# Strassen-type weight sums for the second FFN, made in HBM by accumulating transfers of GpSimd's queue

## The chip, the cores and the metric

The kernel runs on one core of one Trainium2 chip. The metric is the device time of one execution in microseconds (us); several runs are given by their median. TensorE multiplies a stationary operand of 128 x 128 with a moving operand of up to 512 columns into a bank of PSUM. VectorE (DVE), ScalarE (ACT) and GpSimd (POOL) work on tiles of 128 partitions. Transfers are issued by the queues of SyncE (SP), ScalarE and GpSimd and carried out by sixteen DMA engines. Each engine takes its instructions in the order in which the built program has them.

## The reference

Two layers over 256 tokens of width 2048 in float32. Layer 0 mixes tokens by latent attention, layer 1 by dilated attention; each is followed by an FFN whose up projection has 2 x 5632 columns and a causal convolution of width 3.

```python
def conv_ffn(h, w_up, conv_w, conv_b, w_down):
    u = h @ w_up
    up = jnp.pad(u, ((0, 0), (CONV_WIDTH - 1, 0), (0, 0)))
    c = conv_b + up[:, 0:S] * conv_w[0]
    for j in range(1, CONV_WIDTH):
        c = c + up[:, j:j + S] * conv_w[j]
    gate, val = c[..., :FFN_HIDDEN], c[..., FFN_HIDDEN:]
    return (jax.nn.silu(gate) * val) @ w_down

for i in range(DEPTH):
    x = x + (mla_mixer if i % 2 == 0 else dilated_mixer)(rms_norm(x, attn_norm[i]), ...)
    x = x + conv_ffn(rms_norm(x, ffn_norm[i]), ffn_w_up[i], ...)
return rms_norm(x, final_norm)
```

## The kernel before, in words

Activations are kept transposed: 16 chunks `xt[k]` of 128 features by 256 tokens. Every float32 operand is split into a high and a low part (`wh`, `wl` for weights, `xs` for activations), and a product is the sum of three: high by high, low by high, high by low.

A **unit** is one block of 128 output features. `load` brings 1 MB of weights on SP's queue into one of three buffers `w`, ScalarE makes `wh` and VectorE `wl` (tiles of 1024 columns, five buffers each), and `proj` runs 16 matmuls of 512 columns (`wh` by high and low of `xs`) and 16 of 256 (`wl` by the high part). `unit` evacuates the bank of the unit before and takes one entry of `steps`, a list of other work laid between units.

The norm's factor is applied after the product: `rstd_x` sums squares with TensorE, and GpSimd takes the power to -1/2 (`rcol`). `spread` then has TensorE make a table over all partitions from it. In `ffn` the steps `col` and `wide` do so beside the first units; `keep` multiplies by that table, writes the result into one of four padded tiles `upad`, which GpSimd clears at their first two columns, and calls `conv`. In the first mixer, GpSimd also adds the squares of x (`acc`) and takes the powers for the two latent norms (`s`).

The FFN has 44 feature blocks `fb`, each with a gate and a value unit (`up`). Their outputs stay in SBUF for a segment (`SEGS`) of 10 to 12 blocks, then `down` runs 16 units, one for each output chunk, over that segment.

A **four** is a group of four consecutive blocks that is not computed directly. `seven` treats tokens (two halves), input features (two halves) and gate or value as a 2 x 2 x 2 block product and does it with seven products in place of eight, after Winograd's form. The roles are turned: 128 tokens are stationary, and 512 columns of weights move. A product has 8 x 3 matmuls. The stationary sums (`forms`, from `make_forms`) are made once; the weight sums `t13` and `t24` are made on VectorE. Six products advance together, one slice of the input features at a time (`first`, `second`), between the units of a `down`; the seventh (`third`), the sums of the outputs and the transposes back (`turn`) follow as steps of the next units. There are three fours (`SEVEN`, at 12, 23 and 34) in each of the two FFNs.

The built order is not the order of the text: a scheduler places each instruction on its engine by its dependences and by its own estimate of times, within the buffers that are free.

## Time and profile before

| | us |
|---|---|
| three runs | 2674.88, 2675.78, 2676.62 |
| median | 2675.78 |
| profiled execution, first to last instruction (span) | 2673.9 |
| first mixer, up to GpSimd's power for the first FFN's norm | 272 |
| first FFN | 722 |
| second mixer (dilated attention and its output projection) | 951 |
| second FFN | 719 |

Only the span is known of the profiled execution; it lies 1.9 us below the runs' median. The stages are cut at GpSimd's powers, of which there is one for each norm. In the profile, a row of an engine names its line, its operation and its tiles as output<-inputs.

### The profile page before, as it was taken

To read this page: it belongs to the slowest core of one execution; us is meant where nothing else is said; L and a number is where in the kernel's file an instruction comes from. 1 tells how busy PE (TensorE), PEld (TensorE's weight loads), DVE (VectorE), ACT (ScalarE), POOL (GpSimd) and SP (SyncE) were. 2 spreads that over 40 slices of the span, in tenths; PEclk is the share of its full clock that TensorE was granted. 3 is DMA by queue.
4 is the path that set the end of the run, shared out by engine and by line. 5 is a ranking of instruction groups with operands and counts; after the bars stand their busy time and mean duration, and the time that the engine had idled before them with its cause. 6 is when DMAs were issued, how large, how long until landed. Compare 5 with 4: busy or idle time off the path is not lost.

```text
span 2673.9 us, 40017 instructions
## 1 busy us (share of the span) xinstructions
PE 2657.8 (99%) x15167; PEld 2338.4 (87%) x15167; DVE 2105.5 (79%) x3630; ACT 1639.7 (61%) x2624; POOL 24.7 (1%) x39
## 2 busy tenths in 40 slices
PE   9999999999999999999999999999999999999998
PEld 7998888888888888898888888888888888888887
DVE  7987888898898876676577667667688889889885
ACT  6775666676666764444454444445666667666665
POOL 2000000000000000000000000000000000000000
PEclk9999999999999999999999999999999999999999
DMA  6335555656566565544544544544555575755744
GB/s 246 138 133 203 189 182 193 239 179 224 197 202 227 182 206 198 179 171 170 191 170 164 197 161 174 188 174 160 189 189 175 191 249 171 223 205 189 237 169 147
DMA packets 153553, 506.19 MB, mean 189 GB/s; under 512 B 11024, under 2 KB 86160, under 8 KB 118928
## 3 DMA queue, kind: packets, MB, share of 16 engines
q1 hardware_dynamic: 153072, 503.46, 54.9%
q8 instruction: 119, 1.95, 0.3%
q14 instruction: 74, 0.61, 0.1%
q10 hardware_dynamic: 288, 0.18, 0.0%
HBM read 501.50 MB, written 2.10 MB: 188 GB/s over the span
## 4 chain that ended last, share of the span: by engine, by line
PE 95%; DMA 1%; DVE 1%; issue 0%; ACT 0%; SPq 0%; DVEq 0%; ACTq 0%
PE pp L137 70%; PE pp L165 3%; PE pp L167 3%; PE pp L166 3%; PE ps L855 1%; PE ps L853 1%; PE ps L854 1%; DMA w<-in_wup 1%; PE pp L104 1%; PE pp L106 1%; PE pp L105 1%; PE pp L853 1%; PE pp L854 1%; PE pp L855 1%; PE po L781 1%; PE ps L744 1%
## 5 line engine op out<-in xcount | busy, mean ns | idle before, releaser
L92 DVE TENSOR_TENSOR wl<-w,wh 128x1024 fp32r<-128x1024 f32 (+3 forms) x802 | 881.9, 1110 | 371.0 <-ACT wh L91 228.1
L91 ACT ACTIVATE wh<-w 128x1024 fp32r<-128x1024 f32 (+3 forms) x802 | 770.9, 966 | 370.8 <-PE pp L137 220.7
L137 PE MATMUL pp<-xs,wh 128*128 128x512 f32 x3648 | 855.5, 390 | 0.0
L137 PEld LDWEIGHTS pp<-xs,wh 128*128 128x128 f32 x3648 | 677.1, 188 | 135.8 <-DVE xs L266 0.2
L137 PE MATMUL pp<-xs,wl 128*128 128x256 f32 x3648 | 465.3, 284 | 0.0
L137 PEld LDWEIGHTS pp<-xs,wl 128*128 128x128 f32 x3648 | 455.7, 191 | 9.3
L137 PE MATMUL pp<-a,wh 128*128 128x512 f32 x1920 | 459.7, 390 | 0.0
L137 PEld LDWEIGHTS pp<-a,wh 128*128 128x128 f32 x1920 | 357.7, 188 | 72.6
L137 PEld LDWEIGHTS pp<-a,wl 128*128 128x128 f32 x1920 | 248.1, 191 | 10.2
L137 PE MATMUL pp<-a,wl 128*128 128x256 f32 x1920 | 252.8, 283 | 0.0
L155 DVE TENSOR_TENSOR wl<-w,wh 128x1024 fp32r<-128x1024 f32 x96 | 116.2, 1218 | 62.3 <-ACT wh L154 50.3
L154 ACT ACTIVATE wh<-w 128x1024 fp32r<-128x1024 f32 x96 | 101.6, 1059 | 96.5 <-PE pp L166 50.0
L213 ACT ACTIVATE lo<-pp 128x256 f32<-128x256 f32 x225 | 85.7, 381 | 119.5 <-PE pp L137 119.4
L165 PE MATMUL pp<-wh,xs 128*128 128x512 f32 x384 | 150.0, 391 | 0.0
L167 PE MATMUL pp<-wl,xs 128*128 128x512 f32 x384 | 149.5, 389 | 0.0
L166 PE MATMUL pp<-wh,xs 128*128 128x512 f32 x384 | 149.4, 389 | 0.0
L962 DVE SCALAR_TENSOR_TENSOR cv<-upad,convs,cv 128x256 f32<-128x256 f32 x256 | 121.1, 481 | 18.3 <-ACT cv L958 15.9
L958 ACT ACTIVATE cv<-upad,convs 128x256 f32<-128x256 f32 x128 | 76.4, 598 | 72.7 <-DVE upad L972 71.0
L215 DVE TENSOR_TENSOR sum<-pp,lo 128x256 f32<-128x256 f32 x225 | 94.1, 418 | 0.2
L120 ACT ACTIVATE pp<-x 128x512 f32<-128x512 f32 x144 | 85.1, 591 | 13.6 <-DVE sum L215 6.8
L880 ACT ACTIVATE wh<-w 128x1024 fp32r<-128x1024 f32 x48 | 51.0, 1062 | 60.0 <-PE pp L137 43.0
L167 PEld LDWEIGHTS pp<-wl,xs 128*128 128x128 f32 x384 | 72.1, 188 | 15.0
(299 smaller groups left out, 3154.7 us busy)
## 6 DMA issues: line engine op xcount, KB each, us to landing
w<-in_wup SPq DMA_DIRECT2D x128, 1024.0 KB, 4.8
w<-in_win SPq DMA_DIRECT2D x96, 1024.0 KB, 4.8
w<-in_wup SPq DMA_DIRECT2D x96, 512.0 KB, 5.1
w<-in_win SPq DMA_DIRECT2D x96, 512.0 KB, 4.1
w<-in_wdn SPq DMA_DIRECT2D x64, 704.0 KB, 4.1
w<-in_wdn SPq DMA_DIRECT2D x32, 768.0 KB, 4.2
w<-in_wdn SPq DMA_DIRECT2D x32, 640.0 KB, 5.3
w<-in_wo SPq DMA_DIRECT2D x16, 1024.0 KB, 4.7
```

The lines of the kernel that those rows point to most:

```text
L91: nc.scalar.activation(h, w[:, c:e], AF.Copy)
L92: nc.vector.tensor_sub(l, w[:, c:e], h.bitcast(F32))
L120: nc.scalar.activation(dst, chunk.unsqueeze(1).to_broadcast([P, 2, 2, P]), AF.Copy, scale=0.5)
L137: nc.tensor.matmul(ps[:, i * T:], w_k, xs[k][:, :(2 - i) * T], start=(k == 0 and i == own), stop=(k == n - 1), skip_group_check=(i != own))
L154: nc.scalar.activation(wh4, src, AF.Copy)
L155: nc.vector.tensor_sub(wl4, src, wh4.bitcast(F32))
L165: nc.tensor.matmul(ps, xh, wh, start=k == 0, stop=False)
L166: nc.tensor.matmul(ps, xl, wh, start=False, stop=False)
L167: nc.tensor.matmul(ps, xh, wl, start=False, stop=k == KC - 1)
L213: nc.scalar.activation(t, ps[:, T:], AF.Copy)
L215: nc.vector.tensor_add(u, ps[:, :T], t)
L962: nc.vector.scalar_tensor_tensor(o, v, convs[:, cw + j:cw + j + 1], o, op0=ALU.mult, op1=ALU.add)
```

## The change

The second layer's FFN gets a function of its own, `ffn_ahead`, with six fours (24 blocks) in place of three. The form of the sums is changed so that the four weight sums are plain additions: with the unit weights w(h, j), where h is gate (0) or value (1) and j the half of the input features, t1 = w(0,0) + w(1,0), t3 = w(1,1) + w(1,0), t2 = w(1,1) + t1, t4 = w(0,1) + t2. Here j halves the 16 chunks as first and last eight, not as even and odd ones. The signs are carried by the stationary forms and the sums of the outputs.

The weight sums are tiles in HBM. `plan_sums` lists, for each four, 16 copies and 16 accumulating transfers (`accum_op=ALU.add`) of 128 x 1024 elements on GpSimd's queue, 192 in all. In the text of `dilated`, two of them are issued with each load of the second mixer, and what is left ahead of its output projection. The products are run one after the other, each in two halves: a half loads 1 MB, either of plain weights or of a ready sum, splits it on ScalarE and VectorE and runs 24 matmuls. `PERIODS` and `steady` lay the halves between the units of three down segments and some direct blocks; the fourth segment follows the last four.

```diff
+FIRST, LAST = 12, 29
+PERIODS = ((0, 11, 12, (16, 17, 18), 19), (11, 18, 23, (27, 28, 29), 30), (18, 29, 34, (38, 39), 40))
...
+        hbm = ctx.enter_context(tc.tile_pool(name="hbm", bufs=1, space=bass.MemoryType.DRAM))
...
+        def plan_sums(layer, fb0):
+            unit_ = lambda f, h, j: wup_d[layer, 2 * (fb0 + f) + h, :, j * WS:(j + 1) * WS]
+            t = {i: hbm.tile([4, P, WS], F32, name=f"t{i}_{layer}_{fb0}") for i in (1, 2, 3, 4)}
+            made[layer, fb0] = t
+            for i, h, j in ((1, 0, 0), (3, 1, 1), (2, 1, 1), (4, 0, 1)):
+                for f in range(4):
+                    sums_ahead.append(lambda i=i, f=f, h=h, j=j: nc.gpsimd.dma_start(t[i][f], unit_(f, h, j)))
+            for i in (1, 3):
+                for f in range(4):
+                    sums_ahead.append(lambda i=i, f=f: nc.gpsimd.dma_start(t[i][f], unit_(f, 1, 0), accum_op=ALU.add))
+            for i, o in ((2, 1), (4, 2)):
+                for f in range(4):
+                    sums_ahead.append(lambda i=i, o=o, f=f: nc.gpsimd.dma_start(t[i][f], t[o][f], accum_op=ALU.add, max_dma_last_dim=WS))
+
+        def some_sums(n):
+            for _ in range(n):
+                if sums_ahead:
+                    sums_ahead.pop(0)()
...
                             w = load(win_d[base + 2 * i + e], D, tok=D)
+                            if j > 0 or g > 0:
+                                some_sums(2)
                             unit(lambda: proj(w, xs, KC), lambda ps, what=what, g=g, e=e: keep_qk((what, g, e), ps))
...
+            some_sums(len(sums_ahead))
             out_proj(dwo_d, os, G_FFN + KC, onto=True)
...
+        def ffn_ahead(layer, goff, ready):
...
+                def product(i, q):
+                    name, what = products[i]
+                    if q == 0:
+                        ps[i] = pss.tile([P, 512], F32, name="ps", tag="ps")
+                    w = wst.tile([P, D], F32, name="w", tag="w")
+                    if isinstance(what, int):
+                        src = t[what][:, :, q * HALF:(q + 1) * HALF]
+                    else:
+                        h, j = what
+                        src = wup_d[layer, 2 * fb0:2 * fb0 + 8].rearrange("(f i) p c -> i f p c", i=2)[h]
+                        src = src[:, :, j * WS + q * HALF:j * WS + (q + 1) * HALF]
+                    nc.sync.dma_start(w.rearrange("p (f c) -> p f c", f=4), src.rearrange("f p c -> p f c"))
+                    w5 = w.rearrange("p (f k c) -> p k f c", f=4, k=4)
+                    for h in range(2):
...
+                        nc.scalar.activation(as4(wh), w5[:, 2 * h:2 * h + 2], AF.Copy)
+                        nc.vector.tensor_sub(as4(wl), w5[:, 2 * h:2 * h + 2], as4(wh).bitcast(F32))
+                        for k in range(2):
...
+                            nc.tensor.matmul(ps[i], xh, bh, start=(kk == 0), stop=False)
+                            nc.tensor.matmul(ps[i], xl, bh, start=False, stop=False)
+                            nc.tensor.matmul(ps[i], xh, bl, start=False, stop=(kk == KC // 2 - 1))
...
+            for fb in range(FIRST):
+                up(fb)
+            for a, b, one, singles, two in PERIODS:
+                am, a_end = seven(one)
+                bm, b_end = seven(two)
+                slots = steady(am, a_end, bm, 2 * len(singles), before)
+                down(a, b)
+                for fb in singles:
+                    up(fb)
+                before = b_end
+            flush()
+            for move in before:
+                move()
+            down(LAST, FB, True)
+            flush()
...
+            for _, _, one, _, two in PERIODS:
+                plan_sums(1, one)
+                plan_sums(1, two)
             dilated()
...
-            ffn(1, G_FFN + KC, final)
+            ffn_ahead(1, G_FFN + KC, final)
```

How the change moves instructions shows on GpSimd first. This is GpSimd's order before, from the last sum of squares of x in the first mixer to the power for the second mixer; the brackets name the semaphores that a row waits for.

```order
L261 TENSOR_TENSOR acc_227<-acc_227,sq_413 128x256 [waits Activation_49]
L309 TENSOR_TENSOR rcol_536<-ms_534,negh_115 128x2 [waits DVE_49]
L321 TENSOR_TENSOR s2_546<-ms_543,negh_115 128x2 [waits DVE_49]
L321 TENSOR_TENSOR s2_759<-ms_756,negh_115 128x2 [waits DVE_49]
L802 MEMSET upad0_3600 128x2 [waits DMAHW6_49,PE_49,Activation_49]
L802 MEMSET upad1_3602 128x2
L802 MEMSET upad2_3604 128x2
L802 MEMSET upad3_3606 128x2
L309 TENSOR_TENSOR rcol_3656<-ms_3654,negh_115 128x2 [waits DVE_49]
L309 TENSOR_TENSOR rcol_11065<-ms_11063,negh_115 128x2 [waits DVE_49]
```

All ten rows are short, and none waits for a transfer of GpSimd's own queue, which has none. Now the same place on GpSimd, at the power for the first mixer's norm; `t1_1_12` is the sum t1 of layer 1's four at block 12, and DMASW0 to DMASW7 are the eight semaphores of GpSimd's transfers.

```order
L206 DMA t1_1_12_11017<-in_wup 128x1024 [waits DMASW1_49]
L285 TENSOR_TENSOR acc_229<-acc_229,sq_415 128x256 [waits Activation_49]
L206 DMA t1_1_12_11017<-in_wup 128x1024 [waits DMASW2_49]
L333 TENSOR_TENSOR rcol_538<-ms_536,negh_117 128x2 [waits DVE_49]
L206 DMA t1_1_12_11017<-in_wup 128x1024 [waits DMASW3_49]
L206 DMA t3_1_12_11019<-in_wup 128x1024 [waits DMASW4_49]
L206 DMA t3_1_12_11019<-in_wup 128x1024 [waits DMASW5_49]
L206 DMA t3_1_12_11019<-in_wup 128x1024 [waits DMASW6_49]
L345 TENSOR_TENSOR s2_548<-ms_545,negh_117 128x2 [waits DVE_49]
L206 DMA t3_1_12_11019<-in_wup 128x1024 [waits DMASW7_49]
L209 DMA t2_1_12_11018<-t1_1_12_11017 512x256 [waits DMASW0_49]
L209 DMA t2_1_12_11018<-t1_1_12_11017 512x256 [waits DMASW1_49]
```

The transfers for the second FFN have moved to the front of the program, between the first mixer's own instructions on GpSimd; four copies stand ahead of the first square, and 19 transfers ahead of this rcol. Further on, GpSimd's order around the power for the first FFN's norm (row 9 of the order before):

```order
L209 DMA t2_1_34_11034<-t1_1_34_11033 512x256 [waits DMASW2_49]
L209 DMA t2_1_34_11034<-t1_1_34_11033 512x256 [waits DMASW3_49]
L209 DMA t4_1_34_11036<-t2_1_34_11034 512x256 [waits DMASW4_49,DMASW0_49]
L209 DMA t4_1_34_11036<-t2_1_34_11034 512x256 [waits DMASW5_49,DMASW1_49]
L209 DMA t4_1_34_11036<-t2_1_34_11034 512x256 [waits DMASW6_49,DMASW2_49]
L209 DMA t4_1_34_11036<-t2_1_34_11034 512x256 [waits DMASW7_49,DMASW3_49]
L203 DMA t1_1_40_11037<-in_wup 128x1024
L333 TENSOR_TENSOR rcol_3658<-ms_3656,negh_117 128x2 [waits DVE_49]
L203 DMA t1_1_40_11037<-in_wup 128x1024 x3
```

Ahead of this power there are now 161 of the 192 transfers: five fours, and the first copy of the sixth. The upad memsets, ahead of it too, stand behind 108 of them. On TensorE, the spread of this power keeps its place at the end of the first FFN's second unit, where it waits for GpSimd.

The other place is TensorE's at the end of the last four. Before, the transposes (outputs `pt` and `po`) stand among direct units (`xs`):

```order
L137 MATMUL pp<-xs_19786,wl 128x256
L137 MATMUL pp<-xs_19795,wl 128x256
L947 MATMUL pt<-cst,t_25705 128x128 [waits DVE_49,PE_49,Activation_49]
L947 MATMUL pt<-cst,t_25705 128x128
L947 MATMUL pt<-cst,t_25704 128x128 x2
L947 MATMUL po<-cst,t_25705 128x128 [waits DVE_49,PE_49,Activation_49]
L947 MATMUL po<-cst,t_25705 128x128
L947 MATMUL po<-cst,t_25704 128x128 x2
L137 MATMUL pp<-xs_19041,wl 128x256
```

Now they follow the last product (`forms`) at once, with only matmuls of the last down segment (`a`) between:

```order
L904 MATMUL ps<-wh,forms_21427 128x512
L905 MATMUL ps<-wl,forms_21427 128x512
L140 MATMUL pp<-a,wh 128x512 [waits Activation_49]
L140 MATMUL pp<-a,wh 128x512 x7
L949 MATMUL pt<-cst,t_25969 128x128 [waits Activation_49]
L949 MATMUL pt<-cst,t_25969 128x128
L949 MATMUL po<-cst,t_25969 128x128 x2
L140 MATMUL pp<-a,wh 128x512 x3
L140 MATMUL pp<-a,wl 128x256 [waits DVE_49]
L140 MATMUL pp<-a,wl 128x256 x7
L140 MATMUL pp<-a,wh 128x512 [waits Activation_49]
```

What moved here is the last four itself: no direct unit stands behind its products any more, and the down segment behind it needs its blocks 40 to 43.

170 lines of the change are left out of this document (added).

## The prediction

> **What bounds the kernel now.** I read the page first, then busy time by stage, then GpSimd's instructions in order of time, and last TensorE's instructions in one stretch of the second layer's FFN.
>
> ```profile
> span 2673.9 us, 40017 instructions
> PE 2657.8 (99%) x15167; PEld 2338.4 (87%) x15167; DVE 2105.5 (79%) x3630; ACT 1639.7 (61%) x2624; POOL 24.7 (1%) x39
> HBM read 501.50 MB, written 2.10 MB: 188 GB/s over the span
> ```
>
> TensorE is at work 99% of the span, so it is the bound, and every wait of TensorE shows in the time one for one. GpSimd has 39 instructions; the kernel writes almost nothing to HBM.
>
> ```profile
> core 0: us, PE busy (x) PEld busy (x) DVE busy (x) ACT busy (x) POOL busy (x), PEclk, DMA share, GB/s
> 0.00:32.00 32.00, 27.34 (x139) 21.17 (x140) 21.29 (x29) 23.12 (x46) 14.34 (x24) 1.00 0.85 305
> ...
> 1945.00:2664.00 719.00, 718.12 (x3994) 627.49 (x3993) 609.10 (x940) 488.85 (x771) 1.77 (x2) 1.00 0.58 195
> ...
> 0.00:64.19 64.19, 58.19 (x324) 48.48 (x325) 50.12 (x88) 45.82 (x84) 17.14 (x26) 1.00 0.68 245
> 64.19:272.03 207.84, 207.54 (x1511) 196.05 (x1510) 170.19 (x453) 138.96 (x340) 1.79 (x6) 1.00 0.45 161
> 0.00:272.03 272.03, 265.73 (x1832) 244.53 (x1833) 220.31 (x540) 184.78 (x424) 18.93 (x32) 1.00 0.51 181
> 272.03:993.99 721.96, 721.96 (x4019) 632.01 (x4018) 622.57 (x963) 496.20 (x780) 1.61 (x1) 1.00 0.60 202
> ```
>
> The last two columns are the busy share of the sixteen DMA engines and what they moved. Up to 272.03 us, which is the whole first mixer, they were busy 0.51 x 272 = 139 us and moved 181 / 0.51 = 355 GB/s while busy (305 / 0.85 = 359 in the fullest stretch). So 133 us of DMA time are free there.
>
> ```profile
> 44.91 0.82 POOL L309 TENSOR_TENSOR rcol<-ms,negh 128x2 f32<-128x2 f32 x1 [11.63 <-DVE ms L307]
> 50.00 0.69 POOL L321 TENSOR_TENSOR s<-ms,negh 128x2 f32<-128x2 f32 x1 [4.27 <-DVE ms L319]
> 64.19 1.59 POOL L321 TENSOR_TENSOR s<-ms,negh 128x2 f32<-128x2 f32 x1 [13.49 <-DVE ms L319]
> 186.78 0.20 POOL L802 MEMSET upad<- 128x2 f32 x4 [120.99 <-ACT a L352]
> 272.03 1.61 POOL L309 TENSOR_TENSOR rcol<-ms,negh 128x2 f32<-128x2 f32 x1 [85.06 <-DVE ms L307]
> ...
> 277.26 0.61 PE L296 MATMUL po<-cst,rcol 128*128 128x128 f32 x4
> ```
>
> These are GpSimd's powers (the norms' reciprocal roots) and, in the last row, TensorE's spread of the one at 272.03, 5.2 us later. All that GpSimd does is short, and TensorE stands behind it within a few us.
>
> **TensorE in the second FFN.** Prices come from starts, since the durations of pipelined matmuls overlap.
>
> ```profile
> 2126.54 0.40 PE L853 MATMUL pp<-wh,forms 128*128 128x512 f32 x1
> ...
> 2127.93 2.43 PE L137 MATMUL pp<-a,wh 128*128 128x512 f32 x10
> 2130.19 1.36 PE L137 MATMUL pp<-a,wl 128*128 128x256 f32 x10
> 2131.38 0.40 PE L853 MATMUL ps<-wh,xs 128*128 128x512 f32 x1
> ...
> 2134.13 2.43 PE L137 MATMUL pp<-a,wh 128*128 128x512 f32 x10
> ...
> L947 PE MATMUL po<-cst,t 128*128 128x128 f32 x24 | 3.6, 273 | 0.0
> L947 PE MATMUL pt<-cst,t 128*128 128x128 f32 x24 | 3.6, 272 | 0.0
> ```
>
> A direct unit is 16 matmuls of 512 columns (2.26 / 10 = 0.226 us each) and 16 of 256 (1.19 / 10 = 0.119): 5.52 us. A matmul of the products takes (2134.13 - 2131.38) / 12 = 0.229 us. Three fours more turn 24 direct units into 504 product matmuls and 48 transposes: -24 x 5.52 = -132.5, +504 x 0.229 = +115.4, +7.2. That is **-10 us**, all on the path, as TensorE is busy 718.12 of 719 us there.
>
> The sums leave VectorE, where they were hidden. A four now takes 28 passes of 1024 columns on each of VectorE and ScalarE; the old products took 44 and 28, four direct blocks 16 and 16.
>
> ```profile
> L882 ACT ACTIVATE wh<-t 128x1024 fp32r<-128x1024 f32 x24 | 25.3, 1054 | 11.0 <-DVE t L881 9.4 <-PE pp L137 1.5
> L895 DVE TENSOR_TENSOR wl<-t,wh 128x1024 fp32r<-128x1024 f32 x24 | 29.3, 1220 | 3.6 <-ACT wh L894 3.6
> ```
>
> VectorE: 6 x 28 - 3 x 44 - 3 x 16 = -12 passes, -15 us, with 110 us to spare in that stage before; ScalarE +36 passes, +38 us, with 230 to spare. Loads of a four stay near 1 MB per 24 product matmuls, 5.5 us, against 1 MB per direct unit of 5.5 us. SP's loads of the sums wait for transfers that landed over 1000 us before. All this I cost at nothing; if the sums were late there, SP and all loads behind it would stand.
>
> One place is new: the last four (blocks 40 to 43) ends straight ahead of the last down segment, where before it ended among direct units. After the last product, VectorE has the sums of the outputs and, for four blocks, the convolutions and splits:
>
> ```profile
> L962 DVE SCALAR_TENSOR_TENSOR cv<-pt,convs,cv 128x254 f32<-128x254 f32 (+1 forms) x24 | 11.4, 477 | 2.0 <-ACT cv L958 2.0
> L967 DVE TENSOR_TENSOR cv<-cv 128x256 f32<-128x256 f32 x44 | 18.5, 420 | 0.6
> L353 DVE TENSOR_TENSOR a<-cv,a 128x256 fp32r<-128x256 f32 x44 | 18.4, 419 | 0.9 <-ACT a L352 0.9
> ```
>
> 4 x (4 x 0.477 + 0.420 + 0.419) = 11 us, against about 6 us of down matmuls that the order puts between the transposes (22 of 512 columns, 11 of 256). Between 0 (more matmuls slip in) and 10 us lost; I take **+5**.
>
> **The sums on GpSimd's queue.** This decides. The code issues them two per load in the second mixer, but they depend on nothing but each other, and in the built order they stand at the front of the program: 160 of the 192 transfers, five fours complete, and one more stand ahead of the first FFN's rcol (272.03 us above). From the ninth on nearly every one waits for an earlier one to land, and GpSimd's queue is in order, so the rcol waits until all but the last five have landed: 80 copies and 76 accumulations of 128 x 1024 x 4 B = 0.524 MB. TensorE's spread waits for the rcol, every later matmul stands behind it, and the loads stop once their buffers are full. On the way the same holds for the squares of the first projection and the powers at 44.91, 50.00 and 64.19 us, but their waits are part of the same lateness: while TensorE stands, the sums go on.
>
> So the rcol comes when the DMA engines have done 139 us of loads and the 156 transfers. The trace has no transfer from HBM to HBM and no accumulation; its nearest rows are loads and stores:
>
> ```profile
> w<-in_wup SPq DMA_DIRECT2D x128, 1024.0 KB, 4.8
> w<-in_wup SPq DMA_DIRECT2D x96, 512.0 KB, 5.1
> out_y<-x SPq DMA_DIRECT2D x7, 256.0 KB, 2.4
> ```
>
> A store has a price like a load's, so three readings bound the sums, all at 355 GB/s. *Each transfer once*: 156 x 0.524 = 81.8 MB, 230 us; the rcol at 139 + 230 = 369, 97 us late. *Each byte read*: an accumulation reads two operands, 80 x 0.524 + 76 x 1.049 = 121.6 MB, 343 us; 210 us late. *Each HBM byte read or written*: 80 x 1.049 + 76 x 1.573 = 203.4 MB, 573 us; 440 us late. The first is too kind, since an accumulation must read what it adds to; between the other two nothing in the trace decides, and I take the middle, **+325 us**.
>
> The Trainium skill, "DMA: Bandwidth & Descriptors", section "Latency and other measured facts", gives 214 GB/s per direction as the full rate of copies between HBM tensors. If an accumulation cost the same, an estimate by that page is 156 x 2.45 = 382 us and the rcol 249 us late; no run here shows such a copy yet.
>
> The other 36 transfers run in the first FFN beside loads that take 0.60 of the DMA time. Hidden as long as the loads, two buffers ahead, still land in time; cost 0 to 20 us, I take **+5**.
>
> The upad memsets at 186.78 us also move behind 108 transfers; their readers need the rcol first, so nothing is added.
>
> Sum: 2673.9 + 325 - 10 + 5 + 5 = 2999 us for the profiled span; the runs' median of 2675.78 lies 2 us above the span: **3000 us**.
>
> **The rivals.** *GpSimd keeps up (faster).* The sums would have to fit into the 133 us that the DMA engines are free before 272 us: 0.85 us for each of 156, or 615 GB/s on top of the loads. Then only -10 + 5 remain: 2671 us. GpSimd's own 1% speaks for it; that the busiest stretch moved 305 GB/s at a share of 0.85 speaks against. It decides at 0.85 us per transfer.
> The same page of the Trainium skill, section "Issuing engines are not separate DMA queues", says that transfers share the sixteen engines whichever engine issued them; by that rule this rival falls. No row shows two busy queues together.
>
> *Cheap sums.* An accumulation costs one pass, 97 us late: 2676 + 97 - 10 = 2763 us. For it: a store as quick as a load. Against: two reads.
>
> *A chain.* Transfers go nearly one at a time, since the last eight of a four wait on the ones just ahead. At the 5.1 us in which 512 KB landed, 156 take 796 us, 524 late: 3200 us. For it: the waits in the order. Against: up to eight may be under way.
>
> **How the numbers follow.** Forecast (late by 210 to 440 us) 0.67, its own range 2885 to 3136; cheap sums 0.13; a chain or worse 0.15; GpSimd keeps up 0.05. The range for 8 in 10 runs from cheap sums to the chain, 2760 to 3200, and leaves out the faster case and half of the chain's. A change under 0.2% (5.4 us) can't be told from none here: the faster rival's 2671 lies at that bound, so 0.03 faster and 0.02 the same; slower 0.95.
>
> **What would show it.** The first FFN's rcol at about 600 us instead of 272; one wait of TensorE of 150 us or more at the spread of rcol, and shorter ones in the first 70 us; DMA busy near 0.9 until the rcol; over 500 us of GpSimd waits on its own transfers. From the first FFN's first unit on, stages as long as before, and the second FFN some 5 us shorter. I am wrong if the rcol is on time, if the sums' landing takes under 1 us each, or if the second FFN grows because TensorE waits for sums or for the last four.

## The result, and the profile after

The changed kernel takes 2864.82 us (median of four runs, 2864.13 to 2866.63) against 2676.2 for the kernel before beside it: 1.0707 times as long, with an interval of 1.0692 to 1.0722. It is slower by 189 us, where the forecast said 324; the range from 2760 to 3200 holds it.

One sentence of the description of the change has to be put right first: a half of a product runs 12 matmuls, not 24. So 1 MB is loaded for 12 matmuls, 2.75 us, which matters below.

The top of the page of the changed kernel:

```profile
span 2862.4 us, 39814 instructions
...
HBM read 633.62 MB, written 102.76 MB: 257 GB/s over the span
```

The span is 188.5 us longer than before. 100.7 MB more are written to HBM, which is 192 transfers of 0.524 MB: every sum transfer, accumulating or not, writes its bytes once, and 132 MB more are read: these 100.7, and 31.5 of loads in the second FFN (the run without sums, below, reads 532.95).

Busy time by stage, in the columns of the prediction's table (the first column of a row is the stretch in us; the last two are the DMA engines' share and GB/s):

```profile
0.00:93.52 93.52, 64.04 (x339) 53.11 (x339) 50.47 (x88) 46.02 (x86) 39.10 (x56) 0.91 1.03 328
93.52:446.39 352.87, 213.23 (x1522) 201.01 (x1522) 173.97 (x460) 141.66 (x343) 95.33 (x137) 0.80 1.08 293
0.00:446.39 446.39, 277.27 (x1861) 254.12 (x1861) 224.44 (x548) 187.69 (x429) 134.43 (x192) 0.82 1.07 300
2119.84:2852.25 732.41, 718.39 (x3778) 610.46 (x3777) 590.10 (x862) 518.78 (x783) 1.61 (x1) 0.99 0.69 234
```

The stretch that ended at 64.19 us now ends at 93.52, and the whole first mixer, which ended at 272.03, at 446.39: **+174.4 us**, with the DMA engines at a share of 1.07 over it (0.51 before). The share adds up the times of single packets, and packets in flight at once overlap, so it can pass 1: GpSimd's queue alone has 107% in the 136 us before the rcol. The second FFN took 718.85 us before between the same two powers, as this row of the kernel before shows:

```profile
1944.72:2663.57 718.85, 717.97 (x3994) 627.57 (x3993) 609.38 (x940) 489.13 (x772) 1.62 (x2) 1.00 0.58 195
```

Now it takes 732.41: **+13.6 us**, where the forecast had -10 and +5. Between the two losses nearly nothing changed. GpSimd's power for the second mixer's norm comes at 1169.12 us, the one for the second FFN's, with which the row above begins, at 2119.84:

```profile
1169.12 1.64 POOL L333 TENSOR_TENSOR rcol<-ms,negh 128x2 f32<-128x2 f32 x1 [619.50 <-DVE ms L331]
```

The first FFN is 1169.12 - 446.39 = 722.73 us (721.96 before), the second mixer 950.72 (950.73). Where the sums reach TensorE is seen in its waits (engine, line, for whom; us in total, times, longest):

```profile
PE po L320 <- POOL rcol L333: 139.4, 1, 139.4
PE po L320 <- DVE s L346: 16.0, 1, 16.0
```

The first row is the spread of the first FFN's rcol; TensorE's own row has it at the start of that matmul:

```profile
447.57 1.22 PE L320 MATMUL po<-cst,rcol 128*128 128x128 f32 x4 [139.37 <-POOL rcol L333]
```

So TensorE reached this place at 308 us, with the first mixer's lateness of about 30 us behind it, and then stood for 139. GpSimd stands too, for its own transfers to land. These are its waits for them over the whole run, 352 us, of which 272 lie ahead of this rcol:

```profile
POOL t L209 <- DMA t<-t: 150.4, 24, 23.7
POOL t L209 <- DMA t<-in_wup: 59.2, 23, 4.0
POOL t L203 <- DMA t<-in_wup: 56.4, 38, 3.2
POOL t L206 <- DMA t<-in_wup: 48.9, 37, 3.0
POOL t L203 <- DMA t<-t: 36.7, 15, 4.7
```

L203 are the copies, L206 the accumulations of plain weights, L209 those of one sum into another. The end of the last four ahead of the rcol, in GpSimd's order of time (start, duration, and in brackets the idle time before and what ended it):

```profile
403.80 0.83 POOL L206 DMA_DIRECT2D t<-in_wup  x1 [1.20 <-DMA t<-in_wup]
...
414.56 0.81 POOL L206 DMA_DIRECT2D t<-in_wup  x1 [0.44 <-DMA t<-in_wup]
417.19 1.01 POOL L209 DMA_DIRECT2D t<-t  x1 [1.81 <-DMA t<-in_wup]
...
424.65 1.01 POOL L209 DMA_DIRECT2D t<-t  x1 [1.47 <-DMA t<-in_wup]
437.26 1.01 POOL L209 DMA_DIRECT2D t<-t  x1 [11.60 <-DMA t<-t]
...
445.21 1.01 POOL L209 DMA_DIRECT2D t<-t  x1 [1.64 <-DMA t<-t]
...
446.39 1.12 POOL L333 TENSOR_TENSOR rcol<-ms,negh 128x2 f32<-128x2 f32 x1
```

These rows are read by what lets each one start: with eight semaphores in turn, a transfer waits for the landing of the eighth ahead of it. The eight L206 rows (403.80 to 414.56) mark the landings of copies: 10.76 / 7 = **1.54 us each**. The first four L209 rows (417.19 to 424.65) mark the landings of accumulations of plain weights: 7.46 / 3 = **2.49 us**. The last four wait for the landings of the first four L209: 7.95 / 3 = **2.65 us**. TensorE stands here and no load competes. The 11.6 us of waiting in between are no gap of the DMA engines: four L206 and the first L209 land in the 12.6 us from 424.65 to 437.26, 2.5 us each.

The share of the sums in the 446.39 us is 446.39 - 139 of loads = 307 us, 1.97 us for each of 156; 80 x 1.54 + 76 x 2.55 = 317 by the prices just read.

### The profile page after: what moved, and what is told of

Its sections match the earlier page's. It is cut to its first block, busy times and chain, and to the rows that moved or that the text cites. A ratio compares the mean times of both kernels' runs of the same rounds, so it can differ in the third digit from the quotient of the medians.

```text
span 2862.4 us, 39814 instructions
## 1 busy us (share of the span) xinstructions
PE 2667.5 (93%) x14951; PEld 2327.5 (81%) x14951; DVE 2085.6 (73%) x3552; ACT 1667.4 (58%) x2635; POOL 162.0 (6%) x231
## 3 DMA queue, kind: packets, MB, share of 16 engines
q0 software_dynamic: 46080, 100.68, 14.9%
HBM read 633.62 MB, written 102.76 MB: 257 GB/s over the span
## 4 chain that ended last, share of the span: by engine, by line
PE 74%; DMA 18%; DVE 4%; ACT 2%; issue 1%; POOL 1%; SPq 0%; DVEq 0%; ACTq 0%; POOLq 0%
PE pp L140 54%; DMA t<-in_wup 8%; DMA t<-t 5%; PE pp L168 3%; PE pp L169 3%; PE pp L170 3%; DMA w<-in_wup 2%; DMA w<-t 2%; PE ps L905 1%; PE ps L903 1%; PE ps L904 1%; DVE wl L898 1%; DVE wl L95 1%; ACT wh L897 1%; DMA w<-in_wqa 1%
## 5 line engine op out<-in xcount | busy, mean ns | idle before, releaser
L95 DVE TENSOR_TENSOR wl<-w,wh 128x1024 fp32r<-128x1024 f32 (+1 forms) x738 | 823.0, 1125 | 378.0 <-ACT wh L94 230.1
L94 ACT ACTIVATE wh<-w 128x1024 fp32r<-128x1024 f32 (+1 forms) x738 | 717.0, 976 | 364.6 <-PE pp L140 205.6
L140 PE MATMUL pp<-xs,wh 128*128 128x512 f32 x3264 | 769.7, 391 | 0.0
L140 PEld LDWEIGHTS pp<-xs,wh 128*128 128x128 f32 x3264 | 607.0, 188 | 121.9 <-DVE xs L290 0.2
L140 PE MATMUL pp<-xs,wl 128*128 128x256 f32 x3264 | 418.6, 284 | 0.0
L140 PEld LDWEIGHTS pp<-xs,wl 128*128 128x128 f32 x3264 | 410.3, 192 | 8.8
L898 DVE TENSOR_TENSOR wl<-w,wh 128x1024 fp32r<-128x1024 f32 x168 | 202.0, 1221 | 39.2 <-ACT wh L897 34.2
L897 ACT ACTIVATE wh<-w 128x1024 fp32r<-128x1024 f32 x168 | 173.4, 1055 | 70.5 <-DMA w<-t 27.8
L158 DVE TENSOR_TENSOR wl<-w,wh 128x1024 fp32r<-128x1024 f32 x96 | 116.2, 1218 | 62.7 <-ACT wh L157 50.6
L157 ACT ACTIVATE wh<-w 128x1024 fp32r<-128x1024 f32 x96 | 101.6, 1058 | 97.2 <-PE pp L169 49.1
L1224 ACT ACTIVATE cv<-upad,convs 128x256 f32<-128x256 f32 x64 | 38.2, 598 | 179.5 <-DVE upad L1238 178.9
L237 ACT ACTIVATE lo<-pp 128x256 f32<-128x256 f32 x201 | 76.5, 381 | 103.8 <-PE pp L140 103.6
```

The source lines that it names most:

```text
L94: nc.scalar.activation(h, w[:, c:e], AF.Copy)
L95: nc.vector.tensor_sub(l, w[:, c:e], h.bitcast(F32))
L140: nc.tensor.matmul(ps[:, i * T:], w_k, xs[k][:, :(2 - i) * T], start=(k == 0 and i == own), stop=(k == n - 1), skip_group_check=(i != own))
L157: nc.scalar.activation(wh4, src, AF.Copy)
L158: nc.vector.tensor_sub(wl4, src, wh4.bitcast(F32))
L237: nc.scalar.activation(t, ps[:, T:], AF.Copy)
```

## Experiments

**What the sums cost, and where.** The first kernel leaves the sums out.

```diff
-                    if isinstance(what, int):
-                        src = t[what][:, :, q * HALF:(q + 1) * HALF]
-                    else:
-                        h, j = what
+                    if True:
+                        h, j = t[what] if isinstance(what, int) else what
...
```

> The sums are not made: no transfer of GpSimd's queue is left, and a product that wants a sum loads a slice of the plain weights of the same size (so its output is another). Six fours by seven products, their order and their loads in the second FFN stay as in the changed kernel. Theory: all of the +174 us up to the first FFN's rcol is the sums' doing and goes; what the second FFN lost (+13.6 us, -12.8 by the count of matmuls and some 26 of stalls) stays, since it comes from the lumps of product halves and the last four's junction and not from where the sums lie: 2676 + 14 = 2690 us. Rival A, that reading sums that accumulating transfers wrote costs the second FFN something by itself: then its 732 us fall towards 706, and the time to 2664. Rival B, that six fours disturb the front by their other changes too: then the rcol comes later than 275 us, and the time is over 2695.

2688.14 us, 1.0055 times before (1.004 to 1.0071). All of the loss at the front is gone (the first FFN's rcol is at 271.87 us), and the second FFN's stays:

```profile
1945.57:2674.55 728.98, 716.49 (x3778) 609.06 (x3777) 589.92 (x862) 518.37 (x783) 1.61 (x2) 1.00 0.69 235
```

728.98 us, 10.1 more than before, without any sum: it isn't reading them that costs most of it. Both rivals fall. (The -12.8 in this text is the forecast's -10, counted with the median distance of all starts of that stage.)

The second kernel makes all sums, later:

```diff
-                    sums_ahead.pop(0)()
+                    tc.keep_in_program_order(sums_ahead.pop(0)())
```

> The same 192 transfers with the same data, but each is held behind what the text has ahead of it on GpSimd, so all of them stand behind the power of the second mixer's norm (about 994 us), at their place in the second mixer. Theory (the price was the order on an in-order queue, not the transfers): the rcol of the first FFN is back at 272 us, the transfers run beside the second mixer in 192 x 1.6 to 2.0 = 310 to 380 us, and the second mixer, whose loads leave the DMA engines free for about 0.45 of its 950 us, hardly grows: 2690 us, with 0 to 15 more for contention. Rival (the transfers take DMA time and HBM rate from the loads wherever they stand): the second mixer grows by a large part of the 174 us: 2780 us or more. A second rival: GpSimd's power for the second FFN's norm or the first loads of sums are late; then TensorE has one wait of over 20 us at 1945 us or behind it.

2686.95 us, 1.0042 (1.0026 to 1.0059): as fast as without sums. The second mixer and the second FFN by stretches:

```profile
994.29:1946.36 952.07, 951.28 (x5321) 833.32 (x5320) 648.13 (x1181) 466.80 (x650) 140.19 (x198) 1.00 0.91 283
...
1946.36:2676.52 730.16, 716.80 (x3778) 609.06 (x3777) 589.58 (x862) 519.05 (x783) 1.64 (x2) 1.00 0.69 235
```

GpSimd's last sum transfer, in its order of time:

```profile
1662.69 1.01 POOL L209 DMA_DIRECT2D t<-t  x1 [3.98 <-DMA t<-t]
```

And the second mixer's loads, from the page's DMA issues (the last column is the median time to landing, 4.8 us before):

```profile
w<-in_win SPq DMA_DIRECT2D x96, 1024.0 KB, 8.5
```

The same 192 transfers take 667 us here from the first issue to the last (995.9 to 1662.7, 3.5 us each, beside the loads), about twice the 310 to 380 us that the text gave, and the loads land later, but all this costs only 952.07 - 950.73 = 1.3 us of TensorE's time. So the 174 us are a matter of place. Whether the place on GpSimd's queue or the place among the loads is for the next kernel, which leaves the sums at the front and takes all other work off GpSimd:

```diff
-            nc.gpsimd.tensor_tensor(r, ms, negh, op=ALU.pow)
+            nc.vector.reciprocal(ms, ms)
+            nc.scalar.activation(r, ms, AF.Sqrt)
...
-                squares(xt[k], k, "x", nc.gpsimd)
+                squares(xt[k], k, "x")
...
-                nc.gpsimd.memset(u[:, 0:2], 0.0)
+                nc.vector.memset(u[:, 0:2], 0.0)
```

> The sums stay at the front of GpSimd's queue as in the changed kernel, but nobody waits for GpSimd's other work any more: the norms' powers are made by a reciprocal of VectorE and a square root of ScalarE, and the squares' adds and the clearing of upad are VectorE's. Theory (TensorE waits because the rcol stands behind the sums in the queue): the wait of 139 us at the spread is gone, the sums end at about 370 to 450 us beside the loads, the start-up stage loses a few us to contention, and the time is 2690 to 2720 us. Rival (the sums crowd out the loads by themselves, and the order on GpSimd only shows it): the loads of the first 450 us are late, TensorE waits for the weights instead, and the time stays within 40 us of 2865.

2831.39 us, 1.0582 (1.0566 to 1.0598). My theory missed by more than 100 us, and the rival comes within its 40. The wait at the spread is gone, but only 33 us with it. The first mixer is 43 us longer than before (up to the rcol, now ScalarE's, at 315.3 us) and the first FFN 100 us (to 1137.2 us); the other 13 of the 156 us are the second FFN's. Two stretches of this run (the rest of the first mixer and the first direct units of the first FFN lie in the first, its first four in the second):

```profile
150.00:430.00 280.00, 280.00 (x1811) 255.56 (x1810) 230.23 (x506) 182.32 (x362) 57.10 (x78) 1.00 1.08 318
430.00:620.00 190.00, 113.05 (x496) 90.70 (x494) 80.42 (x114) 61.11 (x98) 42.64 (x58) 0.79 1.07 279
```

TensorE's longest waits in the second of them, on the splits of the first four's products:

```profile
PE ps L1123 <- DVE wl L1151: 34.5, 6, 11.3
PE ps L1121 <- ACT wh L1148: 23.0, 7, 10.5
```

And its loads there, by their issues:

```profile
w<-in_wdn SPq DMA_DIRECT2D x15, 640.0 KB, 15.6
w<-in_wup SPq DMA_DIRECT2D x14, 512.0 KB, 14.1
```

The same loads in the run without sums, in a stretch from 272 to 460 us:

```profile
w<-in_wdn SPq DMA_DIRECT2D x13, 640.0 KB, 5.2
w<-in_wup SPq DMA_DIRECT2D x12, 512.0 KB, 5.0
```

Beside one load of 1 MB per direct unit of 5.5 us, the sums are hidden even at a DMA share of 1.08: TensorE is busy for 280 of 280 us. Where the products and down units of the first four want smaller loads one upon the other, a load lands after 15 us in place of 5, into three buffers, and TensorE stands for 77 of 190 us. It is slow besides: its granted clock is 0.79 there, 1.00 in the stretch before. The powers of the start-up stage come 40 us late as well (the first rcol at 84.2 us in place of 44.7). The loads are late there too: up to that rcol the five of 1 MB named `w<-in_wkva` land after 22.7 us, where the changed kernel has 9.0 and the run without sums 6.1. Part of it may be this edit's own, since VectorE now adds the squares and ScalarE loads its tables 13 times in the run in place of 7; no run parts the two. So the in-order queue makes one long wait of a price that is paid without it too: the sums need DMA time, and up to 620 us the loads leave it only in parts.

The page "DMA: Bandwidth & Descriptors" of the Trainium skill says, in the section "Queues, rings and completion order", that each DMA engine takes turns between its queues packet by packet; that loads slowed threefold beside eight sum transfers fits it, but no run here shows the turns of single packets.

The last of these four reorders the transfers of a four, so that none adds up what stands right ahead of it.

```diff
-            for i, h, j in ((1, 0, 0), (3, 1, 1), (2, 1, 1), (4, 0, 1)):
...
+            copies(1, 0, 0)
+            copies(2, 1, 1)
+            plain(1)
+            copies(3, 1, 1)
+            chained(2, 1)
+            copies(4, 0, 1)
+            plain(3)
+            chained(4, 2)
```

> The sums stay at the front and GpSimd keeps its other work; only the order of the 32 transfers inside a four is changed, so that an accumulation never stands right behind the one it adds up (copies t1, t2, add into t1, copies t3, add t1 into t2, copies t4, add into t3, add t2 into t4). Theory: the rcol comes when the 156 transfers have landed. If the waits for a landing in the chain t1, t2, t4 set the pace (one of 12 to 24 us in each four), five fours gain 12 to 17 us each: rcol at 360 to 385 us instead of 446, time 2780 to 2805. If the DMA engines' throughput sets it (1.6 to 2.6 us per transfer whatever the order), the rcol stays within 15 us of 446 and the time within 15 us of 2865. I hold the second for likelier in the first 300 us, where the loads compete, and the first behind that: 2835 us.

2861.2 us, 1.0694 (1.0678 to 1.071); GpSimd's rcol in order of time:

```profile
441.44 0.74 POOL L344 TENSOR_TENSOR rcol<-ms,negh 128x2 f32<-128x2 f32 x1
```

TensorE's wait for it:

```profile
PE po L331 <- POOL rcol L344: 141.4, 1, 141.4
```

The rcol is 5 us earlier, the wait as long: the waits of the chain cost next to nothing, as DMA throughput sets the pace. My middle value of 2835 was wrong.

**The price of accumulating.** All transfers copy:

```diff
-                    sums_ahead.append(lambda i=i, f=f: nc.gpsimd.dma_start(t[i][f], unit_(f, 1, 0), accum_op=ALU.add))
+                    sums_ahead.append(lambda i=i, f=f: nc.gpsimd.dma_start(t[i][f], unit_(f, 1, 0)))
```

> The changed kernel (2865 us, the first FFN's rcol at 446 us) with its 192 transfers where they are, but none accumulates: those that added now only copy, with the same bytes, rows and waits (so the sums are not sums, and the output is another). If an accumulation has the price of a copy, as the 1.6 us between starts of both suggests, only the rows of 1 KB made t2 and t4 dear, and the rcol stays within 15 us of 446: 2850 to 2865 us. If reading what is added to has its own price (the reading 'each byte read' of the forecast, 343 us for all against 230), 76 transfers of the 156 gain up to 1.5 us each: the rcol at 335 to 390 us, the time 2755 to 2810. I hold the first for likelier.

2778.26 us, 1.0383 (1.0366 to 1.0401); the guess held for likelier was wrong, and the other's ranges hold the time and the rcol. GpSimd's last L209 rows ahead of the rcol:

```profile
344.17 0.63 POOL L209 DMA_DIRECT2D t<-t  x1 [1.67 <-DMA t<-in_wup]
...
348.49 0.62 POOL L209 DMA_DIRECT2D t<-t  x1 [0.51 <-DMA t<-in_wup]
356.60 0.62 POOL L209 DMA_DIRECT2D t<-t  x1 [7.49 <-DMA t<-t]
...
360.45 0.62 POOL L209 DMA_DIRECT2D t<-t  x1 [0.66 <-DMA t<-t]
...
361.60 0.73 POOL L333 TENSOR_TENSOR rcol<-ms,negh 128x2 f32<-128x2 f32 x1
```

Read as above, the L206 now land 4.32 / 3 = 1.44 us apart and the L209 3.85 / 3 = 1.28, where they took 2.49 and 2.65 as accumulations. The rcol comes 446.39 - 361.60 = 84.8 us sooner, 1.1 us for each of 76. The 1.6 us that I had taken for an accumulation's price was the distance between their starts, which is the landing of copies ahead of them. One thing was not held equal: the queue's packets fell from 46080 to 27648, as the copies of one sum into another went in larger rows. That alone can't be the reason, since the L206, whose rows stayed as they were, fell as well.

**Where the second FFN's 10 to 14 us go.** First, even slots for the product halves (sums held back as above):

```diff
...
+                m = (n + start) // 2 - 1
+                moves += [(start + k * (m - start) // len(a), move) for k, move in enumerate(a)]
...
+                moves += [(m + 2 + k * (n - m - 2) // len(b), move) for k, move in enumerate(b)]
```

> The sums are held behind the second mixer's norm as in the run with the sums held back (2687 us), and the product halves of the second FFN are laid evenly over the slots of a period (one or two in each), where the changed kernel put up to four in a slot of the first two periods and twelve in the last slot of the third. Theory: by the count of matmuls the second FFN is 12.8 us shorter than before, and most of what it lost (it is 730 us in the run with the sums held back, 719 before) are stalls where several halves stand back to back, each of them 1 MB of loads and two splits on VectorE and ScalarE for 2.75 us of TensorE. Even slots take away all but the junction of the last four (about 7 us): 2670 to 2675 us, as fast as before or up to 0.2% faster. Rival: it is the mean load that is too high, not the lumps (14 MB for each four instead of 10): then the time stays within 5 us of 2687.

2684.5 us, 1.0033 (1.0021 to 1.0046): 2.5 us gained of some 15 expected: with three buffers, even slots alone don't give the time back. The next kernel has the even slots too, and changes two things more: the last period is laid out anew, and the order inside a four is the one tried above.

```diff
-PERIODS = (..., (18, 29, 34, (38, 39), 40))
+PERIODS = (..., (18, 29, 34, (), 38))
+BEHIND = (42, 43)
...
+            for fb in BEHIND:
+                up(fb)
             flush()
-            for move in before:
-                move()
```

> As the run with even slots and the sums held back, with the new order inside a four, and with the last period laid out anew: the last four is at block 38, and the direct blocks 42 and 43 run behind it, beside the sums of its outputs and its transposes, so that the last down segment does not wait for them. Theory: the junction's 7 us go too, and what is left is the count: 2664 to 2668 us, 0.3 to 0.4% faster than before. Rival A (the junction costs nothing, the stalls are all in the lumps): the same time as the run with even slots. Rival B (the last period is denser now, 28 halves in 16 slots, and is bound by loads or splits): 3 to 10 us more than the run with even slots.

2685.68 us, 1.0037 (1.0025 to 1.005): as with even slots, so it looked as if rival A held. Two more kernels halve one suspected cost each, without sums:

```diff
-                    w = wst.tile([P, D], F32, name="w", tag="w")
+                    if q == 0:
+                        w = wst.tile([P, D], F32, name="w", tag="w")
...
+                        quarters[i] = w
+                    w = quarters[i]
```

> The run without sums (2688 us), with one load of 1 MB for the two halves of a product in place of two (the second half uses the first half's weights, so its output is another): 42 loads less, everything else, the splits too, as there. Theory: where halves stand back to back the loads set the pace (1 MB at some 355 GB/s takes 2.95 us, a half's matmuls 2.75): with half of them TensorE is fed, and the second FFN falls from 729 us to 715 to 722. Rival (VectorE's and ScalarE's splits set it, 2.44 and 2.11 us in a half of 2.75, behind each other and beside other passes): the time stays within 4 us of 2688.

```diff
-                        wh = wsp.tile([P, WS], F32R, name="wh", tag="wh")
-                        wl = wsp.tile([P, WS], F32R, name="wl", tag="wl")
...
+                        if h == 0:
+                            wh = wsp.tile([P, WS], F32R, name="wh", tag="wh")
+                            wl = wsp.tile([P, WS], F32R, name="wl", tag="wl")
...
```

> The run without sums, with all loads, but with one split into high and low part for each half of a product in place of two (the second two chunks of input features use the first two's parts, so its output is another): 84 passes less on VectorE and on ScalarE, 102 and 89 us of their time. Theory (loads set the pace in the dense stretches): the time stays within 4 us of 2688. Rival (the splits set it): the second FFN falls from 729 us to 715 to 722.

2673.6 us with half the loads (0.9992, 0.9983 to 1.0001) and 2674.58 with half the splits (1.0, 0.9991 to 1.0009). The second FFN with half the loads:

```profile
1945.12:2660.80 715.68, 709.87 (x3778) 611.35 (x3777) 588.15 (x862) 521.68 (x783) 1.62 (x2) 0.99 0.52 178
```

And with half the splits:

```profile
1944.33:2662.07 717.74, 708.75 (x3778) 611.30 (x3777) 496.78 (x778) 440.84 (x699) 1.61 (x2) 1.00 0.70 239
```

Either is enough, 13 and 11 us: the first run bears out the theory that loads set the pace, the second its rival, and neither alone gives both. What loads and splits share is the buffer: it is taken from the issue of a load until VectorE has made the second wl. One turn in the run with even slots, in order of time:

```profile
2305.66 0.37 SPq L891 DMA_DIRECT2D w<-in_wup  x1
...
2310.93 2.01 ACT L897 ACTIVATE wh<-w 128x1024 fp32r<-128x1024 f32 x2 [2.51 <-DMA w<-in_wup]
2312.02 2.36 DVE L898 TENSOR_TENSOR wl<-w,wh 128x1024 fp32r<-128x1024 f32 x2 [0.68 <-ACT wh L897]
...
2314.41 0.34 SPq L81 DMA_DIRECT2D w<-in_wdn  x1
```

Issue at 2305.66, landed 5.3 us later, split until 2314.38, and at 2314.41 SP issues the next load: 8.7 us. It is one turn in a dense stretch; over all 84 halves of that run the median from issue to the end of the second wl is 10.3. That gave the third theory, and two kernels for it:

```diff
-        wst = ctx.enter_context(tc.tile_pool(name="wst", bufs=3))
-        wsp = ctx.enter_context(tc.tile_pool(name="wsp", bufs=5))
+        wst = ctx.enter_context(tc.tile_pool(name="wst", bufs=4))
+        wsp = ctx.enter_context(tc.tile_pool(name="wsp", bufs=4))
```

> The sums held back (2687 us), four buffers w for the loads in place of three, and to make room four buffers each for the high and low parts in place of five. Even slots gained 2.5 us only, and half the loads or half the splits gained 14 us each, so neither rate is the limit alone. New theory: it is the turn of a buffer. In the stretch at 2296 to 2322 us of the run with even slots, a load issued at 2305.66 is ready when ScalarE starts at 2310.93, and VectorE frees the buffer at 2314.38, when the next load is issued: 8.7 us, and with three buffers one load per 2.9 us, where TensorE wants one in 2.65 (a half 2.75, a down unit with 11 blocks about 2.5). With four buffers one per 2.2: TensorE is fed, the second FFN falls from 730 us to 715 to 720, the time to 2672 to 2678. Rival A (the sum of DMA, split and matmul latency is met by nothing but less work): within 4 us of 2687. Rival B: with four buffers for the parts, other stages lose: slower than 2690, the first mixer or the first FFN longer than in the run with the sums held back.

2678.56 us, 1.0012 (1.0002 to 1.0022), the second FFN 719.41 us:

```profile
1945.93:2665.34 719.41, 711.25 (x3777) 610.94 (x3777) 588.17 (x863) 521.59 (x784) 1.62 (x2) 0.99 0.68 237
```

8.4 us gained with the same loads and splits, 10.7 in the second FFN itself: the theory holds, at the upper end of what it gave (the time half a microsecond above it), and the four buffers of the parts cost nothing that shows. The loads show it as well: with three buffers a half's load lands 0.1 us (median) before ScalarE takes it up, with four 2.9 us before. The other kernel loads a product half by two transfers:

```diff
-                    nc.sync.dma_start(w.rearrange("p (f c) -> p f c", f=4), src.rearrange("f p c -> p f c"))
+                    for h in range(2):
+                        part = src[:, :, h * HALF // 2:(h + 1) * HALF // 2]
+                        nc.sync.dma_start(w[:, ts(h, WS)].rearrange("p (f c) -> p f c", f=4), part.rearrange("f p c -> p f c"))
...
```

> The sums held back (2687 us), and the load of 1 MB for a product half is made by two transfers of half a megabyte, each with the input features of one split (its rows are of 1 KB in place of 2). Theory of the buffer's turn: ScalarE can start when the first half has landed, some 1.5 to 2 us sooner, so the turn is 7 in place of 8.7 us and three buffers give a load in 2.3 us: the second FFN 715 to 722 us, the time 2673 to 2680. Rival: rows of 1 KB take the DMA engines longer (GpSimd's accumulations with such rows took 2.6 us against 1.6 of the others, at the spread's wait): the loads land later and the time is 2690 us or more.

2685.29 us, 1.0039 (1.0025 to 1.0052): neither. TensorE's waits in it:

```profile
PE po L951 <- DVE cv L969: 3.1, 3, 1.6
...
PE pp L140 <- ACT wh L94: 2.7, 3, 1.3
...
PE ps L907 <- DVE wl L900: 1.6, 5, 0.5
```

The wait for the halves' wl in the run with the sums held back and one transfer:

```profile
PE ps L905 <- DVE wl L898: 5.5, 11, 0.9
```

TensorE's wait for the halves' wl falls from 5.5 to 1.6 us, as a shorter turn would have it, but in its place come waits for the splits of other units (L94) and for the convolutions. The trace shows why little was gained: the turn did not get shorter by the 1.5 to 2 us expected. ScalarE can start earlier, as the first transfer lands after 4.5 us (median) in place of 5.2, but the second lands after 6.0, and from the first issue to the end of the second wl a half takes 10.8 us on average where it took 11.0. So this run does not speak against the theory, nor for it.

Last, four buffers, even slots and the new last period together:

> The sums held back, four buffers w and four for each of the parts (2679 us), even slots, and the last period with its last four at block 38 and the direct blocks 42 and 43 behind it. With four buffers the stalls between the halves are nearly gone, and what is left stands at the junction of the last four: the starts of TensorE's matmuls at 2571 to 2587 us of that run are some 9 us later than their spacing gives, half-speed matmuls behind the waits counted. Theory: with direct matmuls to run beside the transposes and convolutions the junction gives back 6 to 9 us: 2669 to 2673 us, 0.1 to 0.2% faster than before. Rival (the denser last period needs what the junction gave back, as with three buffers, where the same edit gained nothing): 2677 to 2682 us.

2671.61 us, 0.9987 times the kernel before (0.9978 to 0.9996): 3.7 us faster than it, a small margin, but the interval does not reach 1. It lies within the 2669 to 2673 of the theory.

```profile
1945.99:2657.60 711.61, 706.46 (x3778) 608.45 (x3777) 589.85 (x863) 522.25 (x784) 1.62 (x2) 1.00 0.70 240
```

The second FFN is 7.2 us shorter than before. Even slots and the new last period together gained 1.3 us with three buffers (2686.95 to 2685.68, with the new order inside a four) and 7.0 with four (2678.56 to 2671.61). How the 7 us divide between the two is not shown, but part of them is seen at the junction of the run with four buffers, behind its last products:

```profile
2578.60:2588.80 10.20, 7.66 (x24) 5.97 (x25) 6.82 (x17) 4.03 (x10) 0.00 (x0) 0.50 0.01 5
```

TensorE's granted clock is 0.50 for these 10.2 us. The 7.66 us for which it is busy would be about 3.8 at the full clock (an estimate), so some 4 us go there beside the waits. In the last run no such stretch lies in the second FFN.

## Why the prediction was right, and where not

**The sums at the front: the mechanism was right, the size was not.** The rcol came when the loads and 156 transfers were through, at 446 us in place of 600: +174 where the term said +325. The step that failed is "between the other two nothing in the trace decides, and I take the middle". The three readings had given 97, 210 and 440 us late. A copy cost 1.54 us, one pass (the first reading's 230 / 156 is 1.47), an accumulation 2.5 to 2.65, less than two (2.95): "each byte read", 210, was the nearest and still too high, while the first, 97, was too low. Counting reads and writes both, which made the upper end, was out: a copy does both at the price of one. The trace of before could not tell that; the middle gave this reading half the weight.

The Trainium skill's 214 GB/s ("DMA: Bandwidth & Descriptors", section "Latency and other measured facts") would have made each transfer 2.45 us and the lateness 249. The skill has it for other tiles, on the sync and scalar queues; here copies on GpSimd's queue moved 0.524 MB in 1.54 us, 340 GB/s, so the measurement decides against that figure for this case. It was nearer than my middle only because accumulations happen to cost about that much.

**The cause named was half of it.** "GpSimd's queue is in order, so the rcol waits" is what the trace shows, but without that wait the kernel is still 156 us behind the kernel before, 13 of them in the second FFN. The other half, the sum of DMA time, stood in the same step of the forecast, and the runs give it the greater part, with the one reservation that the kernel without the wait also gave VectorE and ScalarE more to do.

**The rivals.** "GpSimd keeps up" would have needed 0.85 us a transfer; it was 1.97. "A chain" would have needed 5.1; the waits of the chain cost 5 us in all. "Cheap sums" (2763) is near what the kernel without accumulation gave, 2778.

**The other 36 transfers (+5).** The first FFN grew by 0.8 us, inside the 0 to 20 that were given.

**The second FFN (-10).** The step that failed is "Loads of a four stay near 1 MB per 24 product matmuls". It is 1 MB per 12 (the description of the change had the same slip), 14 MB for a four in place of 8 for four direct blocks, at a DMA share of 0.69 where it was 0.58. VectorE's fewer passes were of no use, since what TensorE waited for was no engine's rate but the turn of three buffers, which the forecast put at nothing: some 10 us, which a fourth buffer gave back (730.16 to 719.41). That -10 was about right as a count of matmuls is argued only: the last kernel, at -7.2 with some stalls left, fits it.

**The junction (+5, between 0 and 10).** Its removal together with even slots gave 7 us once there were four buffers, so the size fits, but the junction alone was not measured. The forecast counted VectorE's work there; that TensorE would also run at half its clock for some us, it did not have.

**Two misses of opposite sign.** The front came out 151 us below the forecast and the second FFN 19 above it, so that the total was nearer than the front alone is luck.

**What would show it.** One wait of 139 us (150 or more was named), one of 16 within the first 100, a DMA share of 1.07 (0.9), and 352 us of GpSimd's waits for its own transfers (500): all there, the waits smaller, as the sums were cheaper. Two signs came out otherwise. The second FFN was to be 5 us shorter and was 13.6 longer, and its growth because TensorE waits for sums or for the last four was named as a sign of being wrong: it did not wait for the sums, as the run without them shows, but for its weights, and at the last four.

## What to carry to other kernels

Work moved to DMA queues is paid in DMA time at the place where it runs, not where it is written: look up in the built order where it stands, and price it against the free share of that stage; beside steady loads at a share of 0.5 it was free, in a start-up stage and beside short loads it was not. To size a wait on buffers, take the whole turn, from a load's issue to its last reader, over the number of buffers; here half the loads, half the splits or one more buffer each gave back 10 us or more, while the busy shares of the engines showed room everywhere. Stalls can hide one another: two edits that gained 1.3 us with three buffers were worth 7 with four.

## What was not expected of the hardware

An accumulating transfer from HBM to HBM took 2.5 to 2.65 us for half a megabyte where a copy took 1.3 to 1.54, though the profile counts the same bytes for both (633.62 MB read and 102.76 written with and without accumulation), so it does not count a read of what is added to. And after a short wait TensorE can run at half pace for some matmuls, which the waits don't show; TensorE in the run with even slots, behind a wait of 2.07 us:

```profile
2262.84 0.63 PE L905 MATMUL ps<-wl,xs 128*128 128x512 f32 x1
2263.27 0.63 PE L903 MATMUL ps<-wh,xs 128*128 128x512 f32 x1
...
2264.49 0.40 PE L903 MATMUL ps<-wh,xs 128*128 128x512 f32 x1
2264.73 0.39 PE L904 MATMUL ps<-wh,xs 128*128 128x512 f32 x1
```

0.43 us from start to start, and 0.24 further on. The profile's granted clock tells it apart: it is 0.50 from 2261.0 to 2264.4 us. This happens once more in that run's second FFN, from 2592.1 to 2595.5. Ahead of the two stretches TensorE had stood for 2.0 and 1.8 of 3.4 us; cut into pieces of that length, the run has no other piece up to the second stretch with more than 1.3 us of standing. These figures fit a cause in the time stood in such a piece, and not in one wait; no run was made to test it.
